# The opening of a one-core encoder step: one bias matmul, squares on ScalarE, slices that serve two blocks

## The chip, the cores and the metric

The kernel runs on one core of a Trainium2 chip. A core has TensorE (matmuls; PE in the profile, its weight loads PEld), VectorE (DVE), ScalarE (ACT), GpSimd (POOL) and SyncE (SP), whose queue issues all the DMA transfers here. The metric is the device time of one execution in microseconds (us), the median of several runs.

## The reference

One layer of a streaming encoder, for 2048 new frames with 16 leading meta tokens and for 32 frames of a running stream. Cut to what matters here:

```python
n = rmsnorm(h, norm_g)                       # row scale: 1 / sqrt(mean(h*h) + EPS)
q, k, v, z_a, b_g, c_g, u, z_c = split(n @ w_in, 8)     # 1024 -> 8 x 512
# attention: 4 heads, q and k in two halves of 64, v of 128
bias = rel_bias[rel_bucket(k_pos - q_pos)]   # (q, k, head), shared by both halves
a1 = softmax(q1 @ k1.T / 8 + bias);  a2 = softmax(q2 @ k2.T / 8 + bias)     # chunk-causal
lam = exp(sum(lq1 * lk1)) - exp(sum(lq2 * lk2)) + lam_init
o = rmsnorm((a1 - lam * a2) @ v, subln_g) * (1 - lam_init) * silu(z_a)
y_c = silu(z_c) * b_g * conv3(c_g * u)       # short causal convolution
h = h + concat([o, y_c]) @ w_out;  y = rmsnorm(h, final_g)
```

The keys, values and last convolution rows are outputs too.

## The kernel before

**Two-part numbers.** Every large matmul takes its float32 operands as a rounded part and a remainder (`xh` and `xl` for the inputs, `wh` and `wl` for the weights) and adds three products: xh with wh, xl with wh, xh with wl. ScalarE makes the rounded parts (L152, L204), VectorE the remainders of the inputs (L153), VectorE or GpSimd those of the weights (L205). `halved` (L73 to L78) splits an operation for GpSimd into two halves, and all of them carry the line L78.

**The norm.** The scale of the norm is not applied to the inputs but to each projection's result, as it leaves its bank: the tile `rbs[p]` (`rb`) holds the scale of every row of stage p, the same in all 128 partitions. For stage 0, `x_load(0)` loads eight slices of the transposed input (128 features x 560 rows), makes xh and xl of each, squares the slice (L158), adds the squares into two sums (L162), and takes the sum over the features with a matmul by ones into `pss` (L171). `rsqrt` (L176 to L184) turns that into `rb`, in two halves of 280 rows.

**Stages and heads.** Four stages p of 512 rows; stage 0 has 48 more (meta tokens and the running stream), so a projection is done there in two blocks of 272 to 280 columns. Within a stage, for each of the four heads h: `unit_a` projects q, k, v and the gate z (each `proj` loads 512 KB of weights with `w_load`), `attend` does the scores (L446, L447), the softmax, the transposes and the product with the values, and `unit_c` one quarter of the convolution branch. After the last stage come the output products (L685, L693).

**Banks.** `ps_j` has two banks for projections, `ps_s` three for scores, `ps_t` two, `ps_o` one. In stage 0, values use `ps_s`, all other projections `ps_j`. A bank is free again when its result has been read: for a projection by an `ev_` function, which needs `rb`.

**Buffers.** The tiles of `g_tile` share eight buffers: the eight slices of x, the Toeplitz tables, and results of projections. Weights before rounding have two buffers, `wh` and `wl` four halves each.

**The bias.** `bias_rows` (L594) makes, for each head, one row of 383 biases in all 128 partitions (a matmul of a 32-row one-hot table by a column of `rel_bias`, spread over 128 columns: `pv`, L601), and ScalarE negates it into `bvec` (L603). `prep_small` (L606) writes each to memory (`bd`), reads it back with a row step shorter by one (a Toeplitz table, `g<-bd`), adds the mask (L615), and writes the table to memory (`bz<-g`), from where each head loads it (`bz<-bz`); VectorE adds it to the scores at L393. `prep_small` also computes lambda (L618 to L638), which the softmax's coefficients need (L367, L376).

**What sets the order.** The program is written in the order of the functions called from L741 on, but the instructions of each engine are put in order by a planner at build time: it runs its own clock of all engines, and takes for each the ready instruction that comes first in the program; those under `tc.high_priority()` come ahead of the others. The order is then fixed: on the chip each engine works through its list, and the SyncE queue through its own.

Of the kernel before, what the change touches and what calls it, by code (L numbers as in the profile page):

```python
# [11 lines left out]
F32 = mybir.dt.float32  # L12
F32R = mybir.dt.float32r
AF = mybir.ActivationFunctionType
ALU = mybir.AluOpType
AX = mybir.AxisListType

P = 128
D = 1024
KT = D // P  # L20
# [5 lines left out]
H = 4  # L26
# [7 lines left out]
LV = WIN + P - 1  # L34
NP = (12, 6)
# [12 lines left out]
def hybrid_step(ctx: ExitStack, tc: tile.TileContext, x, xT, ckT, cv, scT, rel_bias, norm_g, w_in,  # L48
# [8 lines left out]
    pp = pool("pp", 1)  # L57
# [15 lines left out]
    def halved(out, a, b, op, engine=None):  # L73

        n = out.shape[-1] if len(out.shape) == 2 else out.shape[1]
        cuts = (0, n // 2, n) if engine is None and n * (out.shape[-1] if len(out.shape) > 2 else 1) > 256 else (0, n)
        for c0, c1 in zip(cuts, cuts[1:]):
            (engine or G).tensor_tensor(out[:, c0:c1], a[:, c0:c1], b[:, c0:c1], op=op)  # L78
# [54 lines left out]
    def sqt(k, n):  # L133

        if k == 0:
            sqs[:] = [f32(t_)[:, 560 * j:560 * (j + 1)] for t_ in [ks_tile(c) for _ in range(2) for c in range(2)] for j in range(3)]
        return sqs[k][:, :n]
# [3 lines left out]
    def x_load(p):  # L141
        c0 = 0 if p == 0 else NX + QT * p
        tw = NX + QT if p == 0 else QT
        if p == 0:
            acc = [None, None]
        for k in range(KT):
            xt = g_tile(tw) if p == 0 else one.tile([P, QT], F32, tag="xt", name="xt", bufs=XB)
            dma(xt, xT[P * k:P * (k + 1), c0:c0 + tw])
            xh[k] = xp.tile([P, NX + QT], F32R, tag=f"xh{k}", name=f"xh{k}")
            xl[k] = xp.tile([P, NX + QT], F32R, tag=f"xl{k}", name=f"xl{k}")  # L150
            with tc.high_priority():
                S.activation(xh[k][:, :tw], xt, AF.Copy, scale=ng[:, k:k + 1])  # L152
                V.scalar_tensor_tensor(xl[k][:, :tw], xt, ng[:, k:k + 1], f32(xh[k][:, :tw]),  # L153
                                       op0=ALU.mult, op1=ALU.subtract)
            if p == 0:
                i = (1, 0, 1, 0, 1, 0, 0, 0)[k]
                sq = sqt(k, tw)
                (halved(sq, xt, xt, ALU.mult) if i else S.activation(sq, xt, AF.Square))  # L158
                if acc[i] is None:
                    acc[i] = sq  # L160
                else:
                    (G if i else V).tensor_tensor(acc[i], acc[i], sq, op=ALU.add)  # L162
        if p == 0:
            rb = one.tile([P, NX + QT], F32, tag="rb", name="rb")
            for i in range(2):
                c = slice(280 * i, 280 * (i + 1))
                var, w = (pp.tile([P, 512], F32, tag="p1", name="xv", bufs=NP[1])[:, :280] for _ in range(2))
                ps = ps_t.tile([P, 2, 256], F32, tag="pt", name="pss").rearrange("p a b -> p (a b)")[:, :280]
                parts = [a[:, c] for a in acc if a is not None]
                for j, a in enumerate(parts):  # L170
                    T.matmul(ps, lhsT=ones, rhs=a, start=(j == 0), stop=(j == len(parts) - 1))  # L171
                with tc.high_priority():
                    rsqrt(rb[:, c], ps, var, w, 1.0 / D)
            rbs[0] = rb

    def rsqrt(r, ssum, var, w, scale):  # L176

        V.tensor_scalar(var, ssum, scale, EPS, op0=ALU.mult, op1=ALU.add)
        S.activation(r, var, AF.Ln)
        S.activation(r, r, AF.Exp, scale=-0.5)  # L180
        V.tensor_tensor(w, r, r, op=ALU.mult)
        V.tensor_tensor(w, w, var, op=ALU.mult)
        V.tensor_scalar(w, w, -0.5, 1.5, op0=ALU.mult, op1=ALU.add)
        V.tensor_tensor(r, r, w, op=ALU.mult)  # L184
# [24 lines left out]
    def proj(col, p, evac):  # L209
        w2 = pre.pop((col, p), None) or w_load(col, p)  # L210
        if p > 0:
            blks = [(0, QT)]
        elif col < CK or CZ <= col < CC or col >= CG:
            blks = [(NM, 288), (288, 560)]
        else:
            blks = [(0, 280), (280, 560)]
        for b0, b1 in blks:
            if p == 0 and col == CV:
                ps = ps_s.tile([P, 512], F32, tag="s", name="pj")[:, :b1 - b0]
            else:  # L220
                ps = ps_j.tile([P, 512], F32, tag="pj", name="pj")[:, :b1 - b0]
            for k in range(KT):
                wh, wl = w2[k // 4]
                for i, (a, b) in enumerate(((wh, xh), (wh, xl), (wl, xh))):
                    T.matmul(ps, lhsT=a[:, k % 4], rhs=b[k][:, b0:b1],  # L225
                             start=(k == 0 and i == 0), stop=(k == KT - 1 and i == 2))
            evac(ps, b0, b1)


# [364 lines left out]
    def bias_rows():  # L594
        rbt = const.tile([32, H], F32, name="rbt")
        dma(rbt, rel_bias)
        oh = pp.tile([P, 512], F32, tag="p1", name="oh", bufs=NP[1])[:32, :LV]
        dma(oh, ohd)
        for h in range(H):
            pv = ps_j.tile([P, 512], F32, tag="pj", name="pv")[:, :LV]  # L600
            T.matmul(pv, lhsT=rbt[:, h:h + 1].broadcast_to([32, P]), rhs=oh, start=True, stop=True)  # L601
            bvec = pp.tile([P, 512], F32, tag="p1", name="bvec", bufs=NP[1])[:, :LV]
            S.activation(bvec, pv, AF.Copy, scale=-1.0)  # L603
            bvs.append(bvec)

    def prep_small():  # L606
        for h in range(H):
            bd = dram.tile([P, LV + 1], F32, name=f"bd{h}", tag=f"bd{h}")
            dma(bd[:, :LV], bvs[h])
            w = g_tile(512)  # L610
            G.memset(w[:, :512 - WIN], 0.0)
            src = bd[:, :]
            toep = bass.AP(tensor=src.tensor, offset=src.offset + P - 1, ap=[[LV, P], [1, WIN]])
            dma(w[:, 512 - WIN:], toep)
            V.tensor_scalar(w[:64, 448:], w[:64, 448:], -NEG, None, op0=ALU.add)  # L615
            bzd.append(dram.tile([P, 512], F32, name=f"bz{h}", tag=f"bz{h}"))
            dma(bzd[h], w)
        lt = g_tile(256).rearrange("p (a d) -> p a d", d=64)  # L618
        dma(lt, lam_in.rearrange("a d -> (a d)").partition_broadcast(P).rearrange("p (a d) -> p a d", d=64))
        V.tensor_tensor(lt[:, 0], lt[:, 0], lt[:, 1], op=ALU.mult)  # L620
        V.tensor_tensor(lt[:, 2], lt[:, 2], lt[:, 3], op=ALU.mult)
        ls = const.tile([P, 2], F32, name="ls")
        V.tensor_reduce(ls[:, 0:1], lt[:, 0], op=ALU.add, axis=AX.X)
        V.tensor_reduce(ls[:, 1:2], lt[:, 2], op=ALU.add, axis=AX.X)
        S.activation(ls, ls, AF.Exp)

        sg = const.tile([P, 2], F32, name="sg")
        V.tensor_tensor(lam2[:, 1:2], ls[:, 1:2], ls[:, 0:1], op=ALU.subtract)
        V.tensor_scalar(lam2[:, 1:2], lam2[:, 1:2], -(0.8 - 0.6), None, op0=ALU.add)
        V.memset(lam2[:, 0:1], 1.0)  # L630
        V.tensor_scalar(sg[:, 0:1], lam2[:, 1:2], -1.0, 1.0, op0=ALU.mult, op1=ALU.max)
        V.tensor_tensor(sg[:, 0:1], sg[:, 0:1], lam2[:, 1:2], op=ALU.max)
        V.reciprocal(sg[:, 1:2], sg[:, 0:1])
        V.tensor_scalar(lam2, lam2, sg[:, 1:2], None, op0=ALU.mult)
        for c in range(2):
            V.tensor_copy(lam_s[NS * c:NS * (c + 1)], lam2[NS * c:NS * (c + 1), c:c + 1])
        V.tensor_tensor(leps, sg[:, 1:2], sg[:, 1:2], op=ALU.mult)
        V.tensor_scalar(leps, leps, EPS, None, op0=ALU.mult)  # L638
# [103 lines left out]
    bias_rows()  # L742
    pre[CQ, 0] = w_load(CQ, 0)
    x_load(0)
    load_small()
    prep_small()
    for p in range(NQ):
        for h in range(H):
            bz = one.tile([P, 512], F32, tag="bz", name="bz", bufs=2)
            if (h, p) != (0, 0):  # L750
                dma(bz, bzd[h])
            st = unit_a(h, p)
            if h == 2 and p < NQ - 1:
                r = x_stats(p + 1)
            if (h, p) == (0, 0):
                dma(bz, bzd[h])
            st["bz"] = bz
            if h == H - 1 and p < NQ - 1:
                x_rms(p + 1, r)
                x_load(p + 1)  # L760
            attend(h, p, st)
            if p == 0:
                attend_sample(h, st)
            for u in after[p == NQ - 1][h]:
                unit_c(u, p)
# [53 lines left out]
```

## Time and profile before

| | |
|---|---|
| median of 3 runs | 1285.72 us (1285.64 to 1286.78) |
| profiled execution: time, span | 1287.04 us, 1285.3 us |
| busy share of the span: TensorE, VectorE, ScalarE, GpSimd | 98%, 72%, 64%, 54% |
| mean granted clock of TensorE | 0.996 |
| HBM traffic | 145.62 MB read, 43.26 MB written |

The profile is one execution, seen by the hardware profiler. A row of the order of time has a start in us from the span's start, a duration in us, the engine, the line of the kernel, the operation, output<-input by the tiles' names, shapes and a count; what stands in brackets is the time the engine was idle before, and what ended that. Matmuls are pipelined, so the time of one is the distance between two starts rather than its duration. A row of stretches has the stretch, its length, the busy time of TensorE (or of the five engines in the order PE, PEld, DVE, ACT, POOL), then the granted clock of TensorE as a share of full speed, the busy share of the DMA engines (about 1 when all are busy) and GB/s. A row of waits has the waiting engine and line, what it waited for, the total in us, how often, and the longest.

### The profile page before, as it was taken

How to read it: one execution, taken by the hardware profiler on the slowest of the kernel's cores; microseconds unless marked ns; L12 is line 12 of the kernel's file. 1: busy time of each engine (PE TensorE's matmuls, PEld its weight loads, DVE VectorE, ACT ScalarE, POOL GpSimd, SP SyncE). 2: the span in 40 equal slices, each digit the busy share in tenths (PEclk: the TensorE clock that was granted, in tenths of full speed). 3: DMA queues.
4: the chain of work that ended last, by engine and by line, in shares of the span. 5: the costliest groups of instructions: out<-in, count | busy, mean ns of one | idle time of the engine just before them, and what ended most of it. 6: DMA issues, size and time to landing. Idle time of an engine off the chain costs nothing.

```text
span 1285.3 us, 21646 instructions
## 1 busy us (share of the span) xinstructions
PE 1264.1 (98%) x7058; PEld 1099.2 (86%) x7058; DVE 921.1 (72%) x2086; ACT 827.9 (64%) x2030; POOL 699.6 (54%) x918
## 2 busy tenths in 40 slices
PE   7999999999999998999999999999999999999997
PEld 6999999988888886888888888888888888888875
DVE  8667566567786847787878667767786896766663
ACT  6745454675776647677767567777777787764331
POOL 5775857767556675455465556454656483443300
PEclk9999999999999999999999999999999999999999
DMA  9744444675435447544353453344335443557752
GB/s 286 231 117 129 141 115 117 209 241 153 133 114 159 139 127 225 168 137 148 99 172 112 144 181 112 126 149 116 108 99 164 164 118 129 189 157 250 231 201 75
DMA packets 108048, 198.74 MB, mean 155 GB/s; under 512 B 17408, under 2 KB 45600, under 8 KB 107936
## 3 DMA queue, kind: packets, MB, share of 16 engines
q1 hardware_dynamic: 107936, 197.37, 49.4%
q8 instruction: 55, 0.90, 0.3%
q14 instruction: 57, 0.47, 0.1%
HBM read 145.62 MB, written 43.26 MB: 147 GB/s over the span
## 4 chain that ended last, share of the span: by engine, by line
PE 59%; DVE 1%; ACT 1%; DMA 0%; issue 0%; DVEq 0%; ACTq 0%
PE pj L225 27%; PE po L693 14%; PE s L446 4%; PE s L447 4%; PE pt L462 4%; PE po L469 2%; PE po L471 2%; PE po L470 2%; PE po L685 1%; DMA xr<-in_x 0%; PE ptv L316 0%; PE pm L474 0%; DVE p L401 0%; ACT p L397 0%; PE pss L423 0%; PE pss L424 0%
## 5 line engine op out<-in xcount | busy, mean ns | idle before, releaser
L78 POOL TENSOR_TENSOR wl<-wr,wh 128x256 fp32r<-128x256 f32 x480 | 376.8, 808 | 302.7 <-ACT wh L204 281.5
L225 PE MATMUL pj<-xh,wh 128*128 128x512 f32 (+2 forms) x1280 | 456.7, 358 | 3.2 <-DVE g L352 1.2
L225 PE MATMUL pj<-xl,wh 128*128 128x512 f32 (+2 forms) x1280 | 452.9, 354 | 1.8 <-DVE xl L153 1.8
L225 PE MATMUL pj<-xh,wl 128*128 128x512 f32 (+2 forms) x1280 | 452.4, 354 | 0.0
L225 PEld LDWEIGHTS pj<-xh,wh 128*128 128x128 f32 x1280 | 242.0, 189 | 35.2 <-issue 2.2
L225 PEld LDWEIGHTS pj<-xl,wh 128*128 128x128 f32 x1280 | 242.0, 189 | 30.7 <-DVE xl L153 2.6
L225 PEld LDWEIGHTS pj<-xh,wl 128*128 128x128 f32 x1280 | 241.6, 189 | 29.9 <-issue 0.2
L397 ACT ACTIVATE p<-s,nm 128x384 f32<-128x384 f32 (+5 forms) x352 | 208.3, 594 | 68.9 <-DVE nm L396 41.8
L204 ACT CAST wh<-wr 128x512 fp32r<-128x512 f32 x256 | 157.4, 618 | 102.5 <-PE pj L225 71.3
L401 DVE SCALAR_TENSOR_TENSOR p<-p,cf,p 128x384 f32<-128x384 f32 (+5 forms) x176 | 126.4, 747 | 24.2 <-ACT p L400 24.0
L396 DVE TENSOR_REDUCE nm<-s 128x1 f32<-128x384 f32 (+3 forms) x224 | 122.6, 560 | 22.8 <-PE s L447 22.5
L466 DVE TENSOR_TENSOR al<-pt,ah 128x512 fp32r<-128x512 f32 x144 | 97.1, 684 | 48.2 <-ACT ah L465 47.8
L78 POOL TENSOR_TENSOR cll<-ct,chh 128x256 fp32r<-128x256 f32 x80 | 64.9, 833 | 118.3 <-ACT chh L671 118.1
L446 PE MATMUL s<-ks,q 128*128 128x384 f32 (+5 forms) x352 | 127.3, 363 | 0.9 <-ACT p L397 0.8
L447 PE MATMUL s<-ks,q 128*128 128x384 f32 (+5 forms) x352 | 122.5, 349 | 0.0
L400 ACT ACTIVATE p<-p,cf 128x384 f32<-128x384 f32 (+5 forms) x176 | 99.1, 623 | 28.3 <-DVE cf L377 25.6
L465 ACT CAST ah<-pt 128x512 fp32r<-128x512 f32 x144 | 81.2, 585 | 43.0 <-PE pt L462 42.0
L393 DVE CUSTOM_DVE_ANT_0 s<-s,bz 128x512 f32<-128x512 f32 (+5 forms) x128 | 74.6, 588 | 22.0 <-PE s L447 19.7
L462 PE MATMUL pt<-ident,p 128*128 128x128 f32 x544 | 86.0, 272 | 0.0
L470 PE MATMUL po<-al,vh 128*128 128x256 f32 x288 | 82.5, 286 | 0.0
L469 PE MATMUL po<-ah,vh 128*128 128x256 f32 x288 | 81.7, 284 | 0.0
L471 PE MATMUL po<-ah,vl 128*128 128x256 f32 x288 | 81.2, 282 | 0.0
(237 smaller groups left out, 2185.4 us busy)
## 6 DMA issues: line engine op xcount, KB each, us to landing
wr<-in_w_in SPq DMA_DIRECT2D x128, 512.0 KB, 3.7
ct<-cat SPq DMA_DIRECT2D x28, 512.0 KB, 4.7
q<-q SPq DMA_DIRECT2D x64, 128.0 KB, 3.0
out<-y SPq DMA_DIRECT2D x32, 256.0 KB, 3.6
ks<-ksd SPq DMA_DIRECT2D x8, 776.0 KB, 5.0
xr<-in_x SPq DMA_DIRECT2D x24, 256.0 KB, 4.6
out<-g SPq DMA_DIRECT2D x24, 256.0 KB, 3.1
xt<-in_xT SPq DMA_DIRECT2D x24, 256.0 KB, 5.2
```

Source lines behind the costliest of these rows:

```text
L78: (engine or G).tensor_tensor(out[:, c0:c1], a[:, c0:c1], b[:, c0:c1], op=op)
L204: S.copy(wh, wi)
L225: T.matmul(ps, lhsT=a[:, k % 4], rhs=b[k][:, b0:b1], start=(k == 0 and i == 0), stop=(k == KT - 1 and i == 2))
L396: V.tensor_reduce(nm[:, c, j:j + 1], s, op=ALU.min, axis=AX.X)
L397: S.activation(pr[j][c], s, AF.Exp, bias=nm[:, c, j:j + 1], scale=-1.0, accum_out=l[:, c, j:j + 1])
L401: V.scalar_tensor_tensor(a0, a1, cf[:, 1, j:j + 1], a0, op0=ALU.mult, op1=ALU.add)
L446: T.matmul(ps, lhsT=qd[c][0][:, qs], rhs=ks[c][:, col:col + w], start=True, stop=False)
L447: T.matmul(ps, lhsT=qd[c][1][:, qs], rhs=ks[c][:, col:col + w], start=False, stop=True)
L462: T.transpose(pt[:, i, P * qi:P * (qi + 1)], cols(aa[qi], NM + P * (2 * j + i), P), ident)
L469: T.matmul(po, lhsT=vh[:, kt], rhs=ah[:, i], start=(kt == 0), stop=False)
L470: T.matmul(po, lhsT=vh[:, kt], rhs=al[:, i], start=False, stop=False)
L693: T.matmul(ps, lhsT=a[k][:, :rows], rhs=b[k], start=(k == 0 and i == 0), stop=(k == KT - 1 and i == 2))
```

## The change

- `bias_rows` makes the rows of all four heads with one matmul into four partitions of one score bank, one negation, and one write to memory; `prep_small` spreads each row over 128 partitions as it writes `bd` from there.
- `x_load(0)` squares every slice on ScalarE; VectorE adds the eight squares, at high priority and behind all eight slices in the program; the sum over the features is one product per half instead of two, at high priority.
- The first query projection takes each slice for both its blocks before the next slice.
- The keys of stage 0 use score banks, as the values do.
- The first key weights are loaded right behind the slices, ahead of `load_small`.
- `prep_small` (tables and lambda) is called behind `unit_a` of the first head instead of before it.

```diff
@@ x_load @@
-            acc = [None, None]
+            sqa = []
...
-                i = (1, 0, 1, 0, 1, 0, 0, 0)[k]
-                sq = sqt(k, tw)
-                (halved(sq, xt, xt, ALU.mult) if i else S.activation(sq, xt, AF.Square))
-                if acc[i] is None:
-                    acc[i] = sq
-                else:
-                    (G if i else V).tensor_tensor(acc[i], acc[i], sq, op=ALU.add)
+                sqa.append(sqt(k, tw))
+                S.activation(sqa[k], xt, AF.Square)
         if p == 0:
             rb = one.tile([P, NX + QT], F32, tag="rb", name="rb")
+            with tc.high_priority():
+                for k in range(1, KT):
+                    V.tensor_tensor(sqa[0], sqa[0], sqa[k], op=ALU.add)
...
-                parts = [a[:, c] for a in acc if a is not None]
-                for j, a in enumerate(parts):
-                    T.matmul(ps, lhsT=ones, rhs=a, start=(j == 0), stop=(j == len(parts) - 1))
                 with tc.high_priority():
+                    T.matmul(ps, lhsT=ones, rhs=sqa[0][:, c], start=True, stop=True)
                     rsqrt(rb[:, c], ps, var, w, 1.0 / D)
@@ proj @@
+        spare = p == 0 and col in (CV, CK)
+        bank = lambda n: (ps_s if spare else ps_j).tile([P, 512], F32, tag="s" if spare else "pj", name="pj")[:, :n]
+
+        def step(ps, b0, b1, k):
+            wh, wl = w2[k // 4]
+            for i, (a, b) in enumerate(((wh, xh), (wh, xl), (wl, xh))):
+                T.matmul(ps, lhsT=a[:, k % 4], rhs=b[k][:, b0:b1],
+                         start=(k == 0 and i == 0), stop=(k == KT - 1 and i == 2))
+        if p == 0 and col == CQ:
+            pss = [bank(b1 - b0) for b0, b1 in blks]
+            for k in range(KT):
+                for ps, (b0, b1) in zip(pss, blks):
+                    step(ps, b0, b1, k)
+            for ps, (b0, b1) in zip(pss, blks):
+                evac(ps, b0, b1)
+            return
         for b0, b1 in blks:
...
+            ps = bank(b1 - b0)
             for k in range(KT):
...
+                step(ps, b0, b1, k)
             evac(ps, b0, b1)
@@ bias_rows @@
-        for h in range(H):
-            pv = ps_j.tile([P, 512], F32, tag="pj", name="pv")[:, :LV]
-            T.matmul(pv, lhsT=rbt[:, h:h + 1].broadcast_to([32, P]), rhs=oh, start=True, stop=True)
-            bvec = pp.tile([P, 512], F32, tag="p1", name="bvec", bufs=NP[1])[:, :LV]
-            S.activation(bvec, pv, AF.Copy, scale=-1.0)
-            bvs.append(bvec)
+        pv = ps_s.tile([P, 512], F32, tag="s", name="pv")[:H, :LV]
+        T.matmul(pv, lhsT=rbt, rhs=oh, start=True, stop=True)
+        bvec = pp.tile([P, 512], F32, tag="p1", name="bvec", bufs=NP[1])[:H, :LV]
+        S.activation(bvec, pv, AF.Copy, scale=-1.0)
+        bvd = dram.tile([H, LV], F32, name="bvd", tag="bvd")
+        dma(bvd, bvec)
+        bvs.extend(bvd[h] for h in range(H))
@@ prep_small @@
-            dma(bd[:, :LV], bvs[h])
+            dma(bd[:, :LV], bvs[h].partition_broadcast(P))
@@ main @@
     bias_rows()
     pre[CQ, 0] = w_load(CQ, 0)
     x_load(0)
+    pre[CK, 0] = w_load(CK, 0)
     load_small()
-    prep_small()
...
             if (h, p) == (0, 0):
+                prep_small()
                 dma(bz, bzd[h])
```

More of the change, by code (lines that the diff above doesn't have):

```diff
@@ L216, in proj @@
             blks = [(0, 280), (280, 560)]
+        spare = p == 0 and col in (CV, CK)
[13 more added lines that the diff above has]
+            return
         for b0, b1 in blks:
[L218 to L221, printed above, removed]
+            ps = bank(b1 - b0)
             for k in range(KT):
[L223 to L226, printed above, removed]
+                step(ps, b0, b1, k)
             evac(ps, b0, b1)
```

## The prediction

> **What bounds the kernel now.** I read four views of the profile: the page's busy shares, the busy time of TensorE by stretches, the list of what TensorE waited for, and the order of time of the first 45 us on each engine.
>
> ```profile
> span 1285.3 us, 21646 instructions
> ...
> PE 1264.1 (98%) x7058; PEld 1099.2 (86%) x7058; DVE 921.1 (72%) x2086; ACT 827.9 (64%) x2030; POOL 699.6 (54%) x918
> ```
> ```profile
> 0.00:20.00 20.00, 13.69 (x52) 1.00 0.87 251
> 300.00:600.00 300.00, 294.79 (x1503) 0.99 0.49 151
> 1240.00:1286.00 46.00, 37.69 (x164) 0.95 0.25 86
> ```
> ```profile
> PE ptv L316 <- DVE g L305: 3.4, 2, 3.2
> PE pj L225 <- DVE xl L153: 1.8, 3, 1.2
> PE pj L225 <- ACT bvec L603: 0.8, 1, 0.8
> PE pj L225 <- DVE g L254: 0.7, 1, 0.7
> ```
> TensorE is busy 1264.1 of 1285.3 us, so 21.2 us of idle time is all that reordering can take from it, beside matmuls that run below full rate. Three stretches hold nearly all of it: 6.3 us in the first 20, 5.2 us between 300 and 600, and 8.3 us in the last 46. The change touches the first. Whatever shortens the opening comes off the end, because TensorE has no slack later to swallow it; that holds if the rest of its order stays as it is.
>
> The opening itself, ScalarE and GpSimd first, then VectorE, then TensorE (columns: start, duration, engine, line, operation, count, idle time before and its releaser):
> ```profile
> 6.97 0.76 ACT L152 ACTIVATE xh<-g,ng 128x560 fp32r<-128x560 f32 x1
> 7.64 0.47 ACT L603 ACTIVATE bvec<-pv 128x383 f32<-128x383 f32 x1
> 14.57 0.66 ACT L158 ACTIVATE ks<-g 128x560 f32<-128x560 f32 x1
> 15.13 0.76 ACT L152 ACTIVATE xh<-g,ng 128x560 fp32r<-128x560 f32 x1
> 15.78 0.67 ACT L158 ACTIVATE ks<-g 128x560 f32<-128x560 f32 x1
> 17.01 1.14 ACT L204 CAST wh<-wr 128x512 fp32r<-128x512 f32 x2 [0.56 <-DMA wr<-in_w_in]
> ```
> ```profile
> 6.87 4.20 POOL L78 TENSOR_TENSOR ks<-g 128x280 f32<-128x280 f32 x4 [5.46 <-DMA g<-in_xT]
> ```
> ```profile
> 8.26 5.25 DVE L153 SCALAR_TENSOR_TENSOR xl<-g,ng,xh 128x560 fp32r<-128x560 f32 x4
> 19.60 0.79 DVE L153 SCALAR_TENSOR_TENSOR xl<-g,ng,xh 128x560 fp32r<-128x560 f32 x1
> 20.31 0.73 DVE L162 TENSOR_TENSOR ks<-ks,ks 128x560 f32<-128x560 f32 x1
> 20.96 1.28 DVE L78 TENSOR_TENSOR wl<-wr,wh 128x512 fp32r<-128x512 f32 x2
> 22.80 0.43 DVE L178 TENSOR_SCALAR xv<-pss 128x280 f32<-128x280 f32 x1
> 29.08 0.44 DVE L184 TENSOR_TENSOR rb<-rb,xv 128x280 f32<-128x280 f32 x1
> ```
> ```profile
> 11.46 0.43 PE L225 MATMUL pj<-xh,wh 128*128 128x272 f32 x1
> 11.69 0.43 PE L225 MATMUL pj<-xl,wh 128*128 128x272 f32 x1
> 20.44 0.39 PE L225 MATMUL pj<-xl,wh 128*128 128x272 f32 x1 [0.35 <-DVE xl L153]
> 21.10 2.15 PE L171 MATMUL pss<-ks,ones 128*128 128x280 f32 x8
> 22.88 0.50 PE L225 MATMUL pj<-xh,wh 128*128 128x280 f32 x1
> 29.11 0.29 PE L225 MATMUL pj<-xh,wl 128*128 128x280 f32 x1
> 30.05 0.40 PE L225 MATMUL pj<-xh,wh 128*128 128x280 f32 x1 [0.66 <-DVE g L254]
> 36.31 0.29 PE L225 MATMUL pj<-xh,wh 128*128 128x272 f32 x1
> ```
> Read from the bottom. The first query projection ends at 21.10 and is released, slice by slice, by the low parts xl from VectorE; its last wait is for the xl that started at 19.60. Then come eight matmuls for the sum of squares (1.78 us to the next start), 48 for the values (6.52 us), a wait of 0.65 us for the first evacuation (keys need a projection bank), 48 for the keys (6.26 us). VectorE is what runs late: it works without a gap from 8.26 to 22. Its first four xl took 1.31 us each while GpSimd squared x slices (four halves in 4.20 us); the last took 0.71 to the next start. An add takes 0.65, a pair of weight low parts 1.28.
>
> **The change part by part.**
>
> *Squares on ScalarE, adds on VectorE.* GpSimd loses six half squares and two adds; nothing waits for it. ScalarE spends 0.65 us on an xh (15.13 to 15.78), 0.56 on a square (14.57 to 15.13), 0.47 on a bias row. Before, eight xh, five squares and three bias rows are 9.4 us; after, eight and eight are 9.7, so its last square ends near 16.7 instead of 16.45: 0.2 us later, off the path. VectorE, with GpSimd out of the way, needs 8 x 0.71 + 7 x 0.65 = 10.2 us for eight xl and seven adds. The first xl can start at 7.9 (weights' low parts at 1.28 a pair, no longer beside GpSimd); the second slice's xh is there at 8.9, and from there seven slices at 0.71 + 0.65 give 18.5 for the last add and 17.85 for the last xl, if adds and xl alternate. If all adds stand behind all xl, the last xl follows ScalarE (16.2 + 0.7 = 16.9), the last add stays near 18.5. Before: 20.4 for that xl and 21.0 for that add.
>
> *Slices serve both blocks.* The trace shows no pile of matmuls left after the last xl even now: from 20.44 to 21.10 both blocks finish. The edit writes down what the planner's order had found; I cost it at nothing, with 0 and +0.7 us (that tail) as ends. The query ends at 17.85 + 0.8 = 18.7.
>
> *One bias matmul.* Three pairs of matmuls and three evacuations at L601 and L603 go. They lie before the slices come, and the projection's start at 10.6 gives way to the pace of the slices: worth nothing on the path, and at most the 0.8 us wait for bvec, which the sum does not count. What is added is a write of the rows to memory: one more issue on the SyncE queue, behind the eight slices (priced under the rivals).
>
> *One matmul for the sum of squares.* VectorE now adds all eight, so two passes of two halves stay instead of eight matmuls: 1.78 becomes 0.89 us.
>
> *Key weights ahead of the small loads, keys in score banks.* The load leaves the SyncE queue before three small transfers, each later by one issue; nobody waits for these for 10 us. ScalarE's 0.56 us wait for that load goes; its cast then starts near 16.7. The keys run before the rows' scale is ready, in two of three score banks, the first value block in the third. The second value block needs the first key block evacuated. The scale took 6.72 us from 22.80 to 29.52, with lambda's small steps between its own; from 19.2 that is 25.9 at the latest, and TensorE comes to that block at 19.6 + 72 x 0.130 = 29.0. The cover is 3.1 us, and the old wait of 0.65 us goes. The keys' low parts are VectorE work (1.28 us for both halves, 0.64 for the first): behind the last add at 18.5 they are there at 19.1, while TensorE does the sum of squares until 19.6.
>
> *Lambda and tables behind the first head.* Twelve table transfers, one for lambda, four GpSimd fills and some twenty small VectorE steps move behind the first head's steps in the program. VectorE has room there:
> ```profile
> 30.05:36.31 6.26, 6.25 (x49) 6.26 (x49) 2.29 (x7) 4.70 (x10) 5.49 (x10) 1.00 1.05 372
> ```
> It is busy (third pair) 2.29 of 6.26 us, so the products cost nothing unless they land ahead of an evacuation.
>
> *Sum.* Queries end at 18.7 instead of 21.1 (2.4), the squares' matmuls save 0.9, the bank wait 0.65: 3.9 us. Ends of that: 1.9, if the keys' weights on VectorE come 2 us later than I place them, and 4.8, if xl stand ahead of adds and the weights ahead of both. The profiled execution took 1287.04 us (1.7 beside its span), 1.3 above the median; 1283.1 for it, 1281.8 for the median.
>
> **A clock that the change could lose.** In the opening the matmuls run at 0.227 us each until about 14.6 (11.46 to 11.69), later at 0.130. Elsewhere the trace shows what a pause does:
> ```profile
> 511.70:515.00 3.30, 0.13 (x2) 0.73 0.94 299
> 515.00:520.00 5.00, 5.00 (x14) 0.50 1.08 377
> ```
> After 3.2 us without matmuls (VectorE behind its queue, L305), the next 5 us run at a granted clock of 0.50, which costs some 2 us more. In the new opening six matmuls per slice at 0.227 are 1.36 us, the slice pace itself, so TensorE stays filled while it is slow and should speed up. The Trainium skill, page "TensorE: Matmul & The Clock Gate", section "HAM oscillation — how this bites in real kernels", says that pauses for data longer than a window of about 3.4 us bring the half rate back each time; section "Part 1: The HAM clock gate" wants about 3.4 us of sustained work to leave it. The trace agrees at 3.2 us. By that rule a slice-paced opening could stay slow.
>
> **The rivals.**
> 1. *The clock stays low through the slices.* Worked out from rows: the last slice's six matmuls take 1.36 instead of 0.78, and 3.4 us of keys run at half rate, 1.7 lost: 2.3 us, so 1284.1. Against it: the pauses between slices (1.37 less 0.78) are far shorter than the 3.2 us above, and the matmuls after today's longest pause for xl, 1.2 us, keep their rate. Chance 0.05.
> 2. *The keys' low parts come late.* Today values run first, with low parts from GpSimd. Now VectorE must make the keys' between adds and scale, at lower priority than both. Behind the whole scale, which took 6.72 us with lambda's steps between its own and takes perhaps half of that without them (an estimate: 3.3 from 19.2), they come at 23.1, and the keys start 0.2 us later than values do today: with the bank wait gone 0.4 gained, 1285.3. It turns slower past 26.1. Chance 0.12.
> 3. *The stall at 511 is dealt anew.* All later order comes from the planner's own clock, which moves with the opening. That stall costs 3.2 + 2.0 = 5.2 us. Gone: 1276.6, chance 0.10. A second one: 1287.0, chance 0.13. For: 5 us lost in one place in 1200 is an accident of order. Against: the heads after the first are the same code.
> 4. *Slower: the bias tables come late.* Head 0's table passes through memory now (the last line but one: time to landing of the transfers that write or read bz):
> ```profile
> 11.29 1.52 SPq L80 DMA_DIRECT2D bd<-bvec  x2
> 16.48 0.89 SPq L80 DMA_DIRECT2D g<-bd  x2
> 24.61 1.03 SPq L80 DMA_DIRECT2D bz<-g  x2
> 33.17 0.58 SPq L80 DMA_DIRECT2D bz<-bz  x1
> DMA to landing us min/median/max: 4.7/6.6/8.0
> 43.52 0.30 DVE L393 CUSTOM_DVE_ANT_0 s<-s,bz 128x144 f32<-128x144 f32 x1
> ```
> It is in place at 37.9 to 41.2 and used at 43.52. After, the use moves to 39.6, and the extra write (issued near 7.5, landing like the others) starts the chain 0.9 to 4.2 us later: from 0.8 early to 5.8 late. VectorE would stand at L393 with evacuations behind it; TensorE can fill one more projection block, 24 x 0.130 = 3.1 us. If the planner also puts the tables 5 us behind the head's transfers, 10.8 late less 3.1, plus 2.0 for the clock, less 3.9, is 5.8 slower: 1291.5. It decides from a lateness of 7.6 us. Chance 0.12.
>
> **How the numbers follow.** Likeliest, 0.48: the sum, 1281.8, by its bounds 1280.9 to 1283.8. A measurement of this kernel tells 0.2% (2.6 us) from no change: below 1283.1 is faster, above 1288.3 slower. Faster: 0.48 + 0.10; the same: 0.05 + 0.12 + 0.13; slower 0.12. The range leaves out the tables' case and most of the vanished stall: 1278.0 to 1288.3.
>
> **What would show it.** Right: the last xl near 17.9 and 0.8 us each, the four squares' matmuls ending near 19.6, keys right behind, no wait for L254, the gate projection starting near 32.4 instead of 36.31, the stall at 511 moved to about 507. Wrong: an idle TensorE before the keys' third matmul (rival 2), matmuls of the keys at 0.23 (rival 1), VectorE waiting at L393 for the table (rival 4), or stretches between 45 and 1240 whose idle time differs from today's 6 us (rival 3).

## The result and the profile after

The changed kernel takes 1294.22 us (median of 5 runs, 1293.47 to 1297.04) against 1285.72 us before in the same session: ratio 1.0065, 95% interval 1.0055 to 1.0076. It is slower by 8.5 us, where 3.9 us of gain were forecast, and it lies above the top of the range, 1288.3. The profiled execution took 1294.21 us. The one before, 1287.04, lies 1.3 us above its median, so the two profiles differ by 7.2 us and not by 8.5. Rows shown together below are picked from one view; others stand between them.

The page of the kernel after:
```profile
span 1292.4 us, 21605 instructions
...
PE 1261.1 (98%) x7048; PEld 1097.9 (85%) x7048; DVE 916.9 (71%) x2089; ACT 828.2 (64%) x2030; POOL 690.8 (53%) x910
```
TensorE works 3.0 us less than before and the span is 7.1 us longer, so idle time grew by 10 us. The stall of VectorE's queue near 511 us serves as a milestone, because the same instruction ends it in every version: the transposition of values on TensorE (`ptv`). It ends in the kernel before at
```profile
514.90 1.11 PE L316 MATMUL ptv<-ident,g 128*128 128x128 f32 x4 [3.17 <-DVE g L305]
```
and in the kernel after at
```profile
522.19 1.11 PE L323 MATMUL ptv<-ident,g 128*128 128x128 f32 x4 [2.83 <-DVE g L312]
```
That is 7.3 us later: the whole loss of this execution lies ahead of the milestone, and the heads behind it run as they did. TensorE's busy time by stretches tells where (start:end, length, busy, granted clock, DMA share, GB/s). Before:
```profile
20.00:40.00 20.00, 19.00 (x140) 1.00 1.02 329
40.00:60.00 20.00, 20.00 (x150) 1.00 0.80 248
60.00:80.00 20.00, 20.00 (x163) 1.00 0.29 54
80.00:100.00 20.00, 19.41 (x148) 1.00 0.66 193
```
After:
```profile
0.00:20.00 20.00, 12.02 (x59) 1.00 0.83 241
20.00:40.00 20.00, 14.09 (x93) 0.83 0.79 265
40.00:60.00 20.00, 18.36 (x145) 1.00 0.75 232
60.00:80.00 20.00, 17.50 (x129) 1.00 0.48 129
80.00:100.00 20.00, 20.00 (x160) 1.00 0.44 131
```
TensorE is idle for 18.0 of the first 100 us, against 7.9 before. Of these 10.1 us more, 5.5 are only work that is gone (bias matmuls 5.89 to 1.43, squares' matmuls 2.15 to 1.10). The other 4.6 are waits, and one stretch runs at half clock (a granted clock of 0.50):
```profile
35.21:39.10 3.89, 3.89 (x17) 0.50 0.91 314
```
Those 17 matmuls follow each other at 0.227 us instead of 0.130, which costs 1.65 us. Together 6.2 of the 7.3; about 1 us stays without a name. What TensorE waited for between 20 and 76 us:
```profile
PE pj L219 <- DVE g L261: 5.9, 1, 5.9
PE pj L219 <- DVE g L546: 1.6, 1, 1.6
PE s L504 <- ACT p L404: 1.5, 1, 1.5
PE pj L219 <- ACT wh L200: 0.8, 1, 0.8
```

**The first wait, 5.9 us.** TensorE stands ahead of the gate projection, which needs the banks of the queries. The evacuations that free them (L261) need the scale `rb`. The chain that makes the scale, on ScalarE, VectorE and TensorE:
```profile
23.65 0.44 ACT L175 ACTIVATE rb<-xv 128x280 f32<-128x280 f32 x1 [3.92 <-DVE xv L174]
27.80 0.63 ACT L115 ACTIVATE xr<-xr 128x512 f32<-128x512 f32 x1 [3.71 <-DMA xr<-in_x]
28.43 0.42 ACT L176 ACTIVATE rb<-rb 128x280 f32<-128x280 f32 x1
```
```profile
17.38 0.80 DVE L153 SCALAR_TENSOR_TENSOR xl<-g,ng,xh 128x560 fp32r<-128x560 f32 x1
23.17 0.45 DVE L174 TENSOR_SCALAR xv<-pss 128x280 f32<-128x280 f32 x1 [3.13 <-PE pss L168]
34.14 0.45 DVE L180 TENSOR_TENSOR rb<-rb,xv 128x280 f32<-128x280 f32 x1
```
```profile
19.26 0.40 PE L219 MATMUL pj<-xh,wh 128*128 128x280 f32 x1 [0.26 <-ACT wh L200]
22.50 1.10 PE L168 MATMUL pss<-ks,ones 128*128 128x280 f32 x4
35.21 0.56 PE L219 MATMUL pj<-xh,wh 128*128 128x272 f32 x1 [5.91 <-DVE g L261]
46.73 0.23 PE L453 MATMUL s<-ks,q 128*128 128x144 f32 x1
```
Between the logarithm (L175) and the exponential (L176) of one half, the planner put a square of the next stage's rows (L115). It needs a load that lands 3.71 us later, and the exponential behind it, ready since 24.1, waits with it. The scale takes from 23.17 to 34.59, 11.4 us instead of 6.72. It also starts late: the keys run from 19.26, but the squares' matmuls start 3.2 us after them, though VectorE had nothing else to do (3.13 us idle). The Trainium skill, page "TensorE: Matmul & The Clock Gate", section "HAM oscillation — how this bites in real kernels", says that a gap longer than about 3.4 us brings the half rate back; the 5.91 us here agree, with 0.50 for the next 3.89 us. As a limit it does not hold here: after the 2.83 us at the milestone the next 5 us read 0.50 too, and the experiments show shorter pauses that did the same.

**The waits between 50 and 75 us: the tables.**
```profile
45.52 0.50 SPq L80 DMA_DIRECT2D g<-bd  x1
```
```profile
54.64 0.19 DVE L623 TENSOR_SCALAR g<-g 64x64 f32<-64x64 f32 x1 [3.73 <-DMA g<-bd]
59.55 0.30 DVE L400 CUSTOM_DVE_ANT_0 s<-s,bz 128x144 f32<-128x144 f32 x1
```
VectorE stands 3.73 us at a table's mask (L623), and evacuations of the convolution branch (L546), which TensorE waits for, stand behind it. Called behind `unit_a`, `prep_small` asks for its tiles among the eight shared `g` buffers after the head has taken them (experiment 5 bears this out). The first table is read at 45.52 instead of 16.48, and the first bias add runs at 59.55 instead of 43.52, 12.8 us behind its scores (46.73). This is the fourth rival, tables that come late and hold evacuations up; the cause is another than its sum had (buffers, not transfers), and VectorE waits at the mask, not at the bias add.

### The profile page after: what moved, and what is told of

It reads as the page before. It is cut to its first block, busy times and chain, and to the rows that moved or that the text cites. A ratio compares the mean times of both kernels' runs of the same rounds, so it can differ in the third digit from the quotient of the medians.

```text
span 1292.4 us, 21605 instructions
## 1 busy us (share of the span) xinstructions
PE 1261.1 (98%) x7048; PEld 1097.9 (85%) x7048; DVE 916.9 (71%) x2089; ACT 828.2 (64%) x2030; POOL 690.8 (53%) x910
## 4 chain that ended last, share of the span: by engine, by line
PE 59%; DVE 1%; ACT 1%; DMA 0%; issue 0%; DVEq 0%; ACTq 0%
PE pj L219 27%; PE po L701 14%; PE s L453 4%; PE s L454 4%; PE pt L469 3%; PE po L476 2%; PE po L478 2%; PE po L477 2%; PE po L693 1%; DMA xr<-in_x 0%; PE ptv L323 0%; PE pm L481 0%; DVE p L408 0%; ACT p L404 0%; PE pss L430 0%; PE pss L431 0%
```

## The experiments

Three edits each take one cause away from the changed kernel. The diffs are cut to their main lines; `tc.issue_after` queues what stands under it behind the instruction named.

**1. The next rows' squares behind the scale** (a_xr).
```diff
-                r = x_stats(p + 1)
+                with tc.issue_after(scale_exp[0].ins):     # the second half's exponential
+                    r = x_stats(p + 1)
```


> The changed kernel with one edit: ScalarE's squares of the next stage's rows (L115) are queued behind the second exponential of the scale. Theory 1 (the scale's chain stood behind a square that waited for its load, 3.7 us of ScalarE idle; and the tables are a second, separate loss): the wait of TensorE before the gate, 5.9 us with about 1.8 us of half clock behind it, goes; the scale is ready near 27.5 instead of 34.6; what the tables cost stays or grows by some of what is won, so 1286 to 1290. Theory 2 (the sum of squares stands 24 matmuls too late in TensorE's order, that is the whole loss): the wait falls by the ScalarE part alone and 3 us or more of it stay, 1290 to 1292. Theory 3 (the tables alone): unchanged, 1294.

Measured 1291.64 us, ratio 1.0045 [1.003, 1.006]. The time lies above theory 1's range and in theory 2's, but the wait is theory 1's: 1.59 us, where theory 2 had 3 or more.
```profile
30.98 0.39 PE L222 MATMUL pj<-xh,wh 128*128 128x272 f32 x1 [1.59 <-ACT wh L203]
31.79 0.43 PE L222 MATMUL pj<-xh,wl 128*128 128x272 f32 x1 [0.29 <-POOL wl L78]
32.02 0.43 PE L222 MATMUL pj<-xh,wh 128*128 128x272 f32 x1
43.78 1.03 SPq L80 DMA_DIRECT2D g<-bd  x1
```
The gate starts at 30.98 instead of 35.21, but the half rate stays: from 31.79 on 16 matmuls follow each other at 0.23 us (a granted clock of 0.53 until 35.3), although the pause was only 1.59 us. A pause of 1.85 us ahead of 51.79 does the same (0.61 from 51.8 to 55.0). Of the 4.2 us, 2.6 reach the end; the tables are still late.

**2. The tables where they were** (a_tab: `prep_small()` ahead of the loop).

> The changed kernel with the tables and lambda called before the first head again. One square of the next stage's rows still stands ahead of the scale's second exponential. Theory 1: the waits between 50 and 75 us (1.6, 0.8, 0.3, 1.5 us) go, the wait before the gate stays at 3 to 6 us with its half clock: 1288 to 1291. Theory 2: as theory 1 within 1 us, it does not speak of the tables. Theory 3: the whole loss goes, 1282 to 1285.

Measured 1289.36 us, 1.0022 [1.0011, 1.0033]: in the range of theories 1 and 2, while theory 3 (the whole loss) fell. The waits between 40 and 80 us are gone (20.00 busy in both stretches). The 4.9 us to the changed kernel are the largest part of the loss that a single edit gave back. A wait at the gate stays. It now ends with the cast of the gate's weights:
```profile
33.16 0.60 PE L219 MATMUL pj<-xh,wh 128*128 128x272 f32 x1 [4.23 <-ACT wh L200]
```

**3. The sum-of-squares matmuls ahead of the keys** (a_pss).
```diff
-        proj(CK + h, p, ev_k)
+        if (h, p) == (0, 0):
+            with tc.issue_after(pss_mm[0].ins):
+                proj(CK + h, p, ev_k)
+        else:
+            proj(CK + h, p, ev_k)
```


> The changed kernel with the first key projection queued behind the two matmuls of the sum of squares on TensorE, so that the sum runs right behind the queries. In the planner's new order a square of the next stage's rows still stands ahead of the second exponential. Theory 1: the chain starts 3 us earlier but ends when the load of those rows lands, near 28 plus 2 to 3 us; the wait before the gate shrinks from 5.9 to between 1 and 4 us, the tables' waits stay: 1289 to 1293. Theory 2: the wait before the gate goes wholly, 1285 to 1288.

Measured 1289.95 us, 1.003 [1.0019, 1.0041], as theory 1 had it. The sum stands at 19.73, the gate starts at 31.17.

**4. Edits 1 and 2, and 1 and 3, together** (a_xr_tab, a_xr_pss).

> Both edits of the two kernels before. Theory 1: both losses gone, and what the prediction summed comes out: 1281 to 1284, faster than the kernel before. Theory 2: 3 us before the gate stay, 1286 to 1288. Theory 3: 1282 to 1285, no better than with the tables alone moved back.

> The changed kernel with ScalarE's squares of the next rows behind the scale's second exponential, and the first key projection behind the two matmuls of the sum of squares; the tables stay late. Theory 1 (with the scale repaired the tables alone set the loss: head 0's table is read from memory only once buffers of the shared eight come free, and its first use stays near 56 us): the gate starts near 31, the wait for the tables takes what that wins, 1288 to 1291, no better than either edit alone (1291.6 and 1290.0). Rival (the opening is what was lost, tables are hidden once it runs): 1282 to 1285.

Measured 1287.81 us, 1.0014 [1.0004, 1.0023], and 1292.01 us, 1.0042 [1.0028, 1.0055]. a_xr_tab missed theory 1's 1281 to 1284 and came out at theory 2's 1286 to 1288; a_xr_pss lies just above its theory's range. The rows of a_xr_tab:
```profile
23.67 0.52 DVE L631 TENSOR_TENSOR g<-g 128x64 f32<-128x64 f32 x1 [3.73 <-DMA g<-in_lam_in]
...
34.03 0.60 PE L222 MATMUL pj<-xh,wh 128*128 128x272 f32 x1 [5.37 <-ACT wh L203]
```
Now lambda's product stands ahead of the scale on VectorE and waits 3.73 us for its load, and the gate waits for weights. In a_xr_pss the scale is done by 25.7, which is the prediction's 25.9, and the gate waits for nothing, yet the scores wait 2.35 us for a copy of q and the tables as ever. Causes in a queue don't add up: the sum of edits 1 and 3 is 6.9 us, both together gave 2.2.

**5. Tables in buffers of their own, behind the scale** (a_own_xr_msk, a_own_xr_pss_msk: edit 1, or 1 and 3, and)
```diff
-            w = g_tile(512)
+            w = pp.tile([P, 512], F32, tag="p0", name="tw", bufs=NP[0])
...
+                with tc.issue_after(scale_exp[1].ins):     # the scale's last product
                     prep_small()
```


> The kernel with the squares behind the exponential (1291.6) and two more edits: the four tables are built in four buffers of the softmax, idle at that time, instead of in the eight shared ones, and their VectorE steps stand behind the scale's last product. Theory 1 (shared buffers made the tables late): the first read of a table moves from 44 us to about 22, the first bias add from 56.5 to about 42, the waits of TensorE between 50 and 75 us go: 1281 to 1284, faster than the kernel before. Rival (the transfers are full, so a table that goes earlier pushes weights back, as the 4.8 us wait of ScalarE for the value weights showed with tables called first): 1286 to 1289.

> The kernel above with the key projection behind the sum of squares as well: all three faults that the traces show are mended, the six parts of the change stand. Theory 1: the scale is ready near 24, the gate starts near 31, tables in time: 1280 to 1284, the predicted 1281.8. Rival (transfers full): 1285 to 1288, with a wait of ScalarE for weights ahead of the gate or of the convolution.

Measured 1287.34 us, 1.0004 [0.9995, 1.0013], and 1286.99 us, 1.0002 [0.9993, 1.0011]: no slower than before, and no faster. The times are the rivals', not the theories' 1280 to 1284. The buffers were the cause of the late tables: with `prep_small` where the change has it, the first bias add comes at 46.6 and 44.2, instead of 56.5 and 58.5 without buffers of their own. In the second kernel the scale is there at 25.95, but VectorE stands at a table's mask (L630) ahead of the queries' evacuation (L264), and not ScalarE at weights, as the rival had it:
```profile
29.08 0.19 DVE L630 TENSOR_SCALAR tw<-tw 64x64 f32<-64x64 f32 x1 [3.14 <-DMA tw<-bd]
...
30.23 0.43 DVE L264 SCALAR_TENSOR_TENSOR g<-pj,rb 128x272 f32<-128x272 f32 x1
```

**6. That mask on GpSimd, and the next rows' squares behind the keys' casts** (a_all_gk).

> The changed kernel with all its orders mended: the sum-of-squares matmuls directly behind the queries, the next rows' squares behind the keys' casts on ScalarE, the tables in buffers of their own and behind the scale's last product, and their masks added on GpSimd instead of VectorE, so that nothing on VectorE waits for a table. Theory (what kept the mended kernels at 1287 was VectorE waiting 3.1 us for the tables ahead of the queries' evacuation): 1281 to 1284 us, no wait over 1 us at the second block of values or at the gate. Rival (the gate's weights land too late whatever the order, the transfers being busy from 20 to 40 us): 1285 to 1287 us, with a wait of 1.5 to 5 us on the gate's weights.

Measured 1289.15 us, 1.0023 [1.0014, 1.0032]: above the ranges of the theory and of the rival. The rival's sign came: the gate waits 2.33 us for low parts of its weights, which stand on GpSimd behind the masks moved there. The rows show new waits in the queues of ScalarE and VectorE:
```profile
33.01 1.14 ACT L203 CAST wh<-wr 128x512 fp32r<-128x512 f32 x2 [4.56 <-DMA wr<-in_w_in]
```
```profile
52.92 0.22 DVE L636 TENSOR_TENSOR g<-g 128x64 f32<-128x64 f32 x1 [4.65 <-DMA g<-in_lam_in]
```
```profile
54.30 0.39 PE L222 MATMUL pj<-xh,wh 128*128 128x280 f32 x1 [2.67 <-DVE g L554]
```
Lambda's product is the newest: it waits 4.65 us for its load, and the evacuation behind it (L554) stops TensorE for 2.67.

**7. The other direction: parts of the change alone in the kernel before.** First the tables (b_tab: only `prep_small` moved behind `unit_a`).

> The kernel before with one part of the change alone: tables and lambda called behind the first head's projections. Theory 1: the tables are read late here too (the first read of a table falls behind the key and value stores), the first bias add moves from 43.5 to 54 to 57 us, and TensorE loses 4 to 8 us between 45 and 75: 1289 to 1294, about the whole loss of the change. Rival (the tables are late only together with the other parts): 1284 to 1287.

Measured 1289.19 us, 1.002 [1.0011, 1.003]: 2.7 us slower, the first bias add at 58.93. The direction was right, the size below the 4 expected. Then the one bias matmul (b_bias), and it with slices and keys (b_slk_bias).

> The kernel before with the one bias matmul alone (four rows by one product, written to memory and read back into all partitions), tables, squares, slices and keys as before. Theory (the opening is paced by x's loads, and the saved matmuls only lengthen an idle time): 1285 to 1286.5 us, queries' end within 0.5 us of before. Rival (the way through memory makes the tables later, or TensorE starts its slices at half rate): 1287 to 1289 us, the first bias add later than 46 us or a wait of 2 us or more between 30 and 60 us.

> b_slk (slices serve both blocks, keys in score banks) with the one bias matmul added. Theory (the bias matmul is neutral): 1283.5 to 1285 us. Rival (it costs what a table or weight load is late by): 1286 to 1288 us.

Measured 1288.45 us, 1.0017 [1.0008, 1.0026], and 1286.29 us, 1.0001 [0.9991, 1.001], both times the rival's range. The part that was priced at nothing costs about 2 us each time. In b_bias:
```profile
21.32 2.15 PE L171 MATMUL pss<-ks,ones 128*128 128x280 f32 x8
24.25 0.40 PE L225 MATMUL pj<-xh,wh 128*128 128x280 f32 x1 [0.78 <-ACT wh L204]
32.07 0.40 PE L225 MATMUL pj<-xh,wh 128*128 128x280 f32 x1 [1.06 <-DVE g L254]
```
```profile
12.47 2.50 SPq L80 DMA_DIRECT2D bd<-bvd  x4
16.88 0.45 SPq L80 DMA_DIRECT2D wr<-in_w_in  x1
```
The queries end no earlier (21.32 against 21.10), so the saved 4.5 us of matmuls only lengthen idle time. The four writes of the rows come as one block of 2.50 us on the SyncE queue, ahead of the load of the third weights, which is issued at 16.88 instead of 14.90. The cast of these weights runs at 23.58, behind the scale's first logarithm on ScalarE, where it ran at 20.48 and ahead of it; TensorE waits 0.78 us for it. How much of that is the load and how much the order is not separated. The scale, with lambda's steps and masks among its own, is ready at 31.5 instead of 29.5, and the wait for the first evacuation grows from 0.66 to 1.06. The first bias add comes at 46.4. The two waits are 1.2 us, about half of the cost; the rest is open.

Last, the opening's own edits: slices alone (b_sl), slices and keys (b_slk), squares and adds (b_sq), all three (b_sqslk).

> The kernel before with the query slices serving both blocks alone, the keys in the projection banks as before. Theory (the keys' bank was worth its 0.66 us wait, the slices the rest of the 2 us): 1284.5 to 1285.3 us. Rival (the planner had interleaved the slices already, and the keys' bank does it all): 1285.8 to 1286.5 us.

> The kernel before with the query slices serving both blocks and the keys in score banks, nothing else; squares and adds stay shared by GpSimd, ScalarE and VectorE. Theory (of the opening's gain, 3.3 us come from the earlier low parts and the halved sum-of-squares matmuls, 0.65 us from the keys' bank): 1285 to 1286 us, queries' end near 21. Rival (the slices by themselves set the queries' end): 1283 to 1284 us.

> The kernel before with only the squares and adds moved (all squares on ScalarE, seven adds on VectorE, one sum-of-squares matmul per half). Theory (the low parts come earlier because GpSimd leaves VectorE alone): last low part near 18, queries' end near 19, 1282 to 1284.5 us. Rival (the queries' end stays at 21 because of the order of the slices, or the gain comes back as a wait at the gate): 1285 to 1287 us.

> The kernel before with the opening's edits alone: squares on ScalarE, seven adds on VectorE, one sum-of-squares matmul per half, query slices that serve both blocks, keys in score banks. The four bias matmuls, the tables and lambda stay as and where they were. In the planned order the sums of squares stand right behind the queries, and the next rows' squares stand behind both halves' exponentials. Theory (the 3.9 us of the prediction's sum are there, and the moved tables, with the order they bring, ate them): 1281 to 1284 us, queries' end near 18.9, TensorE without idle time from 40 to 80 us. Rival (the gain cannot be kept, because the transfers for the gate's weights and the tables land no earlier, and TensorE waits for them instead): 1285 to 1287 us, a wait of 3 us or more on a weight load or a table between 20 and 40 us.

Measured: b_sl 1285.85 us, 0.9999 [0.9991, 1.0008]; **b_slk 1284.17 us, 0.9984 [0.9975, 0.9992]**; b_sq 1285.99 us, 1.0001 [0.9992, 1.001]; b_sqslk 1287.25 us, 1.0009 [1.0, 1.0017]. So b_slk beats both kernels, the one before by 2.0 us (1.0 to 3.2). Its time is nearly the rival's, its queries' end (21.16) the theory's; neither had the reason, since slices without the keys' banks give nothing (b_sl, as its rival had it). Whether the keys' banks give the 2.0 us without the slices was not run. b_sq came out with its rival; b_sqslk lies above its rival's range, with that rival's sign, a wait of 3.1 us. In b_slk
```profile
20.00:40.00 20.00, 20.00 (x152) 1.00 1.02 342
```
TensorE has no gap between 20 and 40 us: with a second projection in score banks, it has matmuls to run while the last slices come (the wait of 1.17 us for an xl shrinks to 0.32) and none waits for an evacuation.

The profiled executions of b_slk (1283.16), b_sq (1283.14) and b_sqslk (1284.59) are the fastest of their runs, so their rows show less than the medians lost. In b_sqslk even there the gate waits, for low parts of its weights that stand on GpSimd behind the keys' low parts:
```profile
33.98 3.45 POOL L78 TENSOR_TENSOR ks<-g,ks 64x140 fp32r<-64x140 f32 x6
37.51 2.89 POOL L78 TENSOR_TENSOR wl<-wr,wh 128x256 fp32r<-128x256 f32 x4
```
```profile
38.38 0.39 PE L219 MATMUL pj<-xh,wl 128*128 128x272 f32 x1 [3.10 <-POOL wl L78]
```

**8. Those low parts planned earlier** (b_sqslk_wl).
```diff
+        if (h, p) == (0, 0):
+            with tc.high_priority():
+                pre[CZ, 0] = w_load(CZ, 0)
         proj(CZ + h, p, ev_z)
```


> b_sqslk with the gate's weight cast and low parts planned early, so that GpSimd makes them ahead of the second half of the keys' low parts. Theory (the 3.1 us wait at the gate was GpSimd's order): the wait falls under 1.6 us and the time to 1284 to 1286 us. Rival (the gate's weights themselves land too late, the transfers being full): the wait stays above 2.5 us and the time at 1286.5 to 1288 us.

Measured 1284.99 us, 0.999 [0.9981, 0.9999]: as the theory had it, and the wait is halved.
```profile
37.00 0.39 PE L219 MATMUL pj<-xh,wl 128*128 128x272 f32 x1 [1.48 <-POOL wl L78]
```

**9. The whole change with nothing in front of anything** (a_early: edits 1 and 3, tables and lambda loaded ahead of the head, their VectorE steps behind the scale; a_early_wl: and edit 8).

> The changed kernel with the tables and lambda back ahead of the first head, but with their VectorE steps queued behind the scale's last product; the sum-of-squares matmuls directly behind the queries, the next rows' squares behind the scale's exponentials. Theory (every loss was a step standing behind a late load, and the opening's 3.9 us are there once none does): 1281 to 1284 us, TensorE without a wait over 1 us between 20 and 80 us. Rival (the transfers, busy without a gap from 20 to 40 us, bring the gate's weights too late for an opening that is 3 us earlier): 1285 to 1287.5 us, with a wait of 1.5 us or more for weights, at the gate or next to it.

> a_early with the gate's weights planned early, so that GpSimd makes their low parts ahead of the queries' second block. Theory (order alone): 1281 to 1284 us, a wait at the gate under 1 us. Rival (the load of the gate's weights sets its start, wherever its cast stands): as a_early within 1 us, and the gate's first wait ends with the load of its weights.

Measured 1287.67 us, 1.0005 [0.9996, 1.0014], and 1286.98 us, 1.0003 [0.9994, 1.0012]. The theory, 1281 to 1284, fell; a_early_wl has its rival's time, and a_early lies 0.2 us above its rival's range. a_early:
```profile
19.43 1.21 PE L168 MATMUL pss<-ks,ones 128*128 128x280 f32 x4 [0.48 <-DVE ks L162]
30.62 0.40 PE L222 MATMUL pj<-xh,wh 128*128 128x280 f32 x1 [0.69 <-DVE g L290]
35.90 0.39 PE L222 MATMUL pj<-xh,wl 128*128 128x272 f32 x1 [1.13 <-POOL wl L78]
...
516.78 1.10 PE L330 MATMUL ptv<-ident,g 128*128 128x128 f32 x4 [3.17 <-DVE g L319]
```
```profile
22.55 1.14 ACT L203 CAST wh<-wr 128x512 fp32r<-128x512 f32 x2 [4.64 <-DMA wr<-in_w_in]
```
The sum-of-squares matmuls start 1.7 us earlier than before (19.43 against 21.10), and the milestone comes 1.9 us later. Of the 3.6 us between, the waits of TensorE that its list shows from 20 to 60 us (3.3 against 1.0 before) are 2.3. The other 1.3 is open, and so is the 0.9 that four sum-of-squares matmuls less should have saved. The largest wait lies on ScalarE: it stands 4.64 us at the cast of the third weights, with the scale's logarithm and exponential behind it. The rival's sign, 1.5 us or more at the gate's weights, did not come in that place, so it is only half confirmed: a late load is behind the largest of these waits, and the loss is spread over several.

## Why the prediction was wrong, step by step

- **Slices, low parts, queries' end, keys' start: right.** The last xl starts at 17.38 and ends at 18.18 (17.85 was the forecast), keys start at 19.26 (19.6 was the forecast). The keys' start is luck: the forecast had them behind the squares' matmuls, and they run ahead of them. The matmuls rose to full rate within the slices (first rival fell), the keys' low parts were in time (second fell), and the stall at 511 only moved (third fell: idle time from 100 us on is the same within 0.3 us). One reading was off, without consequence: the last stretch ends 0.7 us behind the span, so its idle time is 7.6 us and not 8.3.
- **The 2.4 us of the queries' end: present, but not from where I put it, and not kept.** It was credited to squares that leave GpSimd. b_sq ends its queries at 20.41, b_bias at 21.32; the kernel after, which has both edits, near 19. So it takes both: VectorE's pace and the start behind the bias matmuls each hold the slices back. And b_sq, with 0.7 us of it, gained nothing in the median (1.0001); its keys wait 1.69 us for a projection bank, 0.66 before. My sentence "TensorE has no slack later to swallow it" was the error: later loads and the planner's new order swallowed it. The condition that I set, that the rest of the order stays as it is, did not hold.
- **"25.9 at the latest" and the cover of 3.1 us: the step that failed first.** I took the scale's old 6.72 us as an upper bound and let it start at 19.2, right behind the queries. It is a chain over two engines' queues, and a step that the planner places between its parts adds its own wait: it took 11.4 us because of the square that waited for its load, and it began only at 23.17 because the keys' matmuls ran ahead of the sum of squares. The scale was ready at 34.59 instead of 25.9. The cover was exceeded by 5.9 us, plus 1.65 us for the clock.
- **"They cost nothing unless they land ahead of an evacuation" (tables, lambda): failed.** The products cost nothing; the buffers did. I priced the tables' lateness from transfers alone ("0.8 early to 5.8 late") and held the worse case at 0.12. The shared buffers make it 16 us late. Alone in the old kernel that is 2.7 us, in the changed one 4.9. By its number the result lies nearest this rival (1291.5), but it had no part of the loss at the scale.
- **"One bias matmul: worth nothing on the path": mis-sized.** It cost 2.2 us (0.0017, 0.0008 to 0.0026). I counted one added issue. The four writes, now bunched, put a weight load 2 us back, and the planner put the cast of these weights behind the scale's logarithm; 1.2 us of waits are seen, the rest is open.
- **Keys in score banks, 0.65 us, with slices "at nothing": sized too small.** Together 2.0 us, the one part that gains.

The parts measured alone, −2.0 (slices and keys), +2.2 (bias), +2.7 (tables), and +3.2 for the squares on top of slices and keys, come to 6.1 of the 8.5 us. The key weights' earlier load was not run alone; what that load adds and what arises only together make up the rest. The 5.9 us wait, where ScalarE's square stands between the scale's steps, occurs in none of them.

## What to carry to other kernels

In these runs an earlier opening gained only where the loads and steps that the next stage waits for came earlier too; read the issue times of those loads before you count the gain. Where an order is fixed at build time, a chain's old duration is no upper bound: look for what else could be ready on each of its engines, above all steps that wait for a load. Moving a call in the program moves its place in every shared pool of buffers, which can cost more than its instructions. And of a bundle, measure the parts: here two parts alone gained 2 us, and the whole lost 8.5.

## What the runs showed that I had not expected

- The length of a pause alone does not decide whether the half rate follows. Pauses of 1.59 and 1.85 us (a_xr) and 2.83 us (the kernel after, at the milestone) brought it; pauses of 1.64 us (the kernel after, ahead of 55.42) and 3.10 us (b_sqslk, ahead of 38.38) did not: the clock read 1.00 for 3.6 us behind each. What decides is not shown.
- A kernel's runs can scatter by the opening alone: b_sq gave 1283.1 to 1288.8 us in 12 runs. The six above 1286 us have mean granted clocks of 0.993 to 0.995, the six below 0.996 to 0.997. b_slk, without a gap from 20 to 40 us, gave 1283.2 to 1286.1. The 1.69 us pause of b_sq, which in the profiled execution did not bring the half rate, may bring it in others; that is not tested.
- The granted clock of the profile reads 1.00 in the first 20 us even where matmuls follow each other at 0.227 us; the durations show the half rate there, the clock column does not.
